# Token order for every q, k and v product: residue order is made at the splits and, for v, by a copy through DRAM

## The chip, the cores and the metric

The kernel runs on one core of one Trainium2 chip. The metric is the device time of one execution in microseconds; a kernel's time is the median over its runs.

## What is computed

The reference is a trunk of two residual layers on 512 tokens of width 1024, all in float32. Each layer normalises x, multiplies it by a wide matrix `w_in` and cuts the product into the inputs of a recurrent branch (causal convolution, RG-LRU scan, times a GeLU gate), of an attention branch (q, k, v of 12 heads of 128) and of two sigmoid gates. Both branches are projected, gated, summed, projected by `w_out` and added to x. A gated MLP (width 3072, a causal convolution of width 3 before the GeLU) follows.

The attention has three groups of four heads with dilation 1, 4 and 16. Tokens are regrouped by their residue, and inside a residue each query sees a causal window:

```python
def to_blocks(t):
    t = t.reshape(bsz, n, dilation, h, dh).transpose(0, 2, 1, 3, 4)
...
q = rotary(rms_norm(q, q_g), positions) * (HEAD_DIM ** -0.5)
k = rotary(rms_norm(k, k_g), positions)
```

Group outputs are merged by softmax weights from their denominators.

## The kernel before

**Products.** Every product is done as three float32r passes: an operand is split into a high part (rounded, by ScalarE) and a low part (the rest, by VectorE), and `mm3` (lines 258 to 260) multiplies high by high, high by low and low by high into one PSUM bank. x is held transposed as `xh`, `xl` (128 channels by 512 tokens, 8 tiles each). Weights come as 320 units of 128x1024 (`wraw`, 512 KB each, loaded by SP), and each is split into `whi` (ScalarE, line 228) and `wlo` (VectorE, line 233), both with three buffers and two units ahead of TensorE.

**Groups.** A layer's products are a fixed list of groups, each with four PSUM banks `acc`. The first nine are for attention, in the order N1, P1, v0, va, P2, N2, P3, P4, vb, of 4 units and 96 matmuls of 128x512 each. N1 and N2 are q and k of dilation 1, P1 to P4 are q and k of the dilated groups 1 and 2, v0 is v of dilation 1, va and vb are v of the dilated groups. In these nine the x tile is the stationary operand and the weights move ("acc<-whi,xh" in a profile, the moving operand named first); a bank is 128 tokens by 512 channels. In all later groups the weights are stationary ("acc<-xh,whi").

**Which tokens a bank holds.** For N1, N2 and v0 bank b takes tokens 128b to 128b+127. For P1 to P4, va and vb it takes the 128 tokens of residue b modulo 4:

```python
view = "p (r a) -> p r a" if name in IN_ORDER else "p (a r) -> p r a"
av = ah.rearrange(view, r=4)[:, b]
bv = al.rearrange(view, r=4)[:, b]
```

so the stationary operand is 128 neighbouring columns in one case and every fourth column in the other.

**After a q/k group.** `QK.bank` copies each bank to a `slot` (ScalarE). Per bank, `squares` sums the squares of each head (ScalarE), `block` multiplies by the gain, applies rotary with tables `cos`, `sns` (VectorE), scales k by its norm `rs` (two ScalarE activations of 128x128), transposes the four heads into one PSUM tile `at` (TensorE, line 264), and `split` writes the high part (ScalarE) and the low part (VectorE) into the quads `th`, `tl`. The q scale goes into the scores (`rsp` in `score_steps`, VectorE line 237). The tables, the norm `rc` and its form `rcx` exist twice, in token order and in residue order (index `o`).

**After a v group.** `V.bank` scales each bank into a quad `self.t` (ScalarE). `values_perm`, one per head s, splits two residues of va or vb at a time, transposes the probabilities and multiplies ("y<-quad", lines 794 and 795); `values_nat` does it for v0.

**Order of the work.** Engines run their queues in the order written. The order comes from a planner in the kernel: side work (rotary, scores, values, scans, splits) is cut into steps, each with an engine and a time before which it is not put into the queue, and `offer` places steps between the matmuls by running totals of estimated time per engine (`T`). `at` has two buffers; a step that needs one is placed when the estimate says that it came free 500 ns before. A group that needs a result forces what is missing (`ensure`): pa0, the sixth group after vb, needs the attention of each head.

Of the kernel before, what the change touches and what calls it, by code (L numbers as in the profile page):

```python
# [15 lines left out]
F32 = mybir.dt.float32  # L16
# [17 lines left out]
HOP = 6500.0  # L34
# [146 lines left out]
def trunk(tc, wst, lruw, xT, pos, par, gqk, cst, yT):  # L181
    from contextlib import ExitStack
    nc = tc.nc
    with ExitStack() as ctx:
# [151 lines left out]

        def split(hi, lo, src, t=0.0):
            yield need("act", t)
            t = copy(rr(hi), src, t)
            yield need("dve", t)  # L340
            return tt(rr(lo), src, hi, ALU.subtract, t)

# [88 lines left out]
        const = cp.tile([128, C_N], F32, name="const")  # L431
        posi = cp.tile([128, 8], I32, name="posi")
        warm = cp.tile([128, 1], F32, name="warm")
# [16 lines left out]

        cos = cp.tile([128, 8, 64], F32, name="cos")
        sns = cp.tile([128, 8, 2, 64], F32, name="sns")

        def rope_tables():
            yield need("dve", s=3)
            posf = small([8], "posf", 1)
            nc.vector.tensor_copy(posf, posi)
            a, k, r2 = salloc(), salloc(), salloc()
            for r in range(8):
                ts(a[:, r * 64:r * 64 + 64], const[:, C_FR:C_FR + 64], posf[:, r:r + 1], None, ALU.mult)  # L460
                on_dve(60, 0.0)
            magic = float(1.5 * 2 ** 23)
            yield need("dve")
            ts(k, a, float(1.0 / (2 * np.pi)), magic, ALU.mult, ALU.add)
            ts(k, k, -magic, None, ALU.add, dep=T["dve"])
            for p in two_pi_parts():
                yield need("dve", T["dve"])
                stt(a, k, -p, a, ALU.mult, ALU.add, T["dve"])
            yield need("dve")
            lim = 3.1415925  # L470
            t = ts(a, a, lim, -lim, ALU.min, ALU.max)
            yield need("act", t)
            t = act(r2, a, AF.Sin, scale=0.5)
            t = act(sns[:, :, 0, :], a.rearrange("p (r f) -> p r f", r=8), AF.Sin)
# [4 lines left out]
            free(a, k, r2)  # L479

# [63 lines left out]
        def norm_finish(which):  # L544
            yield need("act", s=2, after=[square[c] for c in range(8)])
            sh, sl = salloc(), salloc()
            t = copy(rr(sh), ssq, T["dve"])
            yield need("dve", t)
            t = tt(rr(sl), ssq, sh, ALU.subtract, t)
            yield need("pe", t, at=1)  # L550
            ps = bank()
            nc.tensor.matmul(ps, rr(ones), rr(sh), start=True, stop=False)
            nc.tensor.matmul(ps, rr(ones), rr(sl), start=False, stop=True)
            on_pe(512, 2)
            free(sh, sl)
# [12 lines left out]
            rv = rbc.rearrange("p (a r) -> p r a", r=4)  # L568
            for r in range(4):
                nc.tensor.transpose(pc[:, r:r + 1], rbc[0:1, r * 128:r * 128 + 128], ident[0:1, 0:1])  # L570
                nc.tensor.transpose(pc[:, 4 + r:5 + r], rv[0:1, r, :], ident[0:1, 0:1])
            on_pe(1, 8)
            yield need("dve", T["pe"])
            rc = small([8], "rc", 1)
            nc.vector.tensor_copy(rc, pc[:, 0:8])
            bank_done(on_dve(8, T["pe"]))
            rcx = small([8, 2, 2], "rcx", 1)
            ts(rcx[:, :, 0, :], rc.unsqueeze(2).to_broadcast([128, 8, 2]), -1.0, None, ALU.mult)
            ts(rcx[:, :, 1, :], rc.unsqueeze(2).to_broadcast([128, 8, 2]), 1.0, None, ALU.mult)
            scale["rc"], scale["rcx"] = rc, rcx  # L580
# [4 lines left out]
        class QK:  # L585


            def __init__(self, l, name):
                self.l, self.name = l, name
                self.g, self.left = salloc(), 4  # L590
                nc.sync.dma_start(self.g, gqk[l, list(QK_GROUPS).index(name)].partition_broadcast(128))
                self.msq = small([16], "msq", 2)
                self.o = 0 if name in IN_ORDER else 4
                self.qg = []
                self.rs_done = Chain(None, 0)
# [10 lines left out]
            def squares(self, r):  # L606
                yield need("act", after=(scale["norm"],))
                rc = scale["rc"][:, self.o + r:self.o + r + 1]
                for j in range(4):
                    junk = small([128], "junk", 1)  # L610
                    act(junk, self.qg[r][:, j * 128:j * 128 + 128], AF.Square, scale=rc, accum_out=self.msq[:, 4 * r + j:4 * r + j + 1])

            def chain(self):
# [12 lines left out]
                t = recip(sd, sd, t)  # L626
                self.t_rs = tt(rs, sd, scale["rcx"][:, self.o:self.o + 4], ALU.mult, t)
                self.rs_done.done = True
                yield need("dve", after=subs)

            def block(self, r, after):
                th, tl, rs = qkt[self.name]
                o = self.o + r
                t = self.qg[r]
# [7 lines left out]
                w = t2.rearrange("p (j h f) -> p j h f", j=4, h=2)  # L642
                tt(w, v, sns[:, o].unsqueeze(1).to_broadcast([128, 4, 2, 64]), ALU.mult, e)
                e = tt(v, v, cos[:, o].unsqueeze(1).unsqueeze(1).to_broadcast([128, 4, 2, 64]), ALU.mult, T["dve"])
# [3 lines left out]
                yield need("act", e, after=(self.rs_done,))  # L648
                e = max(e, self.t_rs)
                for j in range(2):  # L650
                    kq = t[:, (2 * j + 1) * 128:(2 * j + 2) * 128]
                    e = act(kq, kq, AF.Copy, e, scale=rs[:, r, 1, j:j + 1])
                yield need("pe", e, at=1)
# [3 lines left out]
                free(t)  # L657
                bl = slice(r * 128, r * 128 + 128)
                bank_done((yield from split(th[:, :, bl], tl[:, :, bl], ps.rearrange("p (j t) -> p j t", j=4), T["pe"])))

        class V:
# [4 lines left out]
            def bank(self, r, ps):  # L666
                o = (0 if self.name in IN_ORDER else 4) + r
                act(self.t[:, r, :], ps, AF.Copy, T["pe"], scale=scale["rc"][:, o:o + 1])

            def end(self):  # L670
                vt[self.name] = self.t
                v_done[self.name].done = True
                v_done[self.name].end = T["act"]

        def score_steps(half, s, p0, p12, st0, st12):
            hq, lq, rsn = qkt["N1" if s < 2 else "N2"]
            hp, lp, rsp = qkt[f"P{s + 1}"]
            yield need("pe", at=1)
# [3 lines left out]
            for b in bs:  # L682
# [9 lines left out]
                else:  # L692
                    for g in range(2):
                        out = ps[:, o + g * 128:o + g * 128 + 128]
                        mm3(out, hp[:, 2 * g, q], lp[:, 2 * g, q], hp[:, 2 * g + 1, q], lp[:, 2 * g + 1, q], True, True)
                        m = C_M1 + 128 * g
                        todo.append((p12[:, b, g * 128:g * 128 + 128], out, rsp[:, b, 0, g:g + 1], const[:, m:m + 128]))
            t = T["pe"]
# [5 lines left out]
            for out, src, r, m in todo:  # L704
                t = stt(out, src, r, m, ALU.mult, ALU.add, t)
            bank_done(t)
# [412 lines left out]
        for l, name, _, nk, k0, _ in GROUPS:  # L1119
# [13 lines left out]
            for uu in range(nk // 2):  # L1133
# [34 lines left out]
                for b in range(4):  # L1168
                    bs = slice(b * 128, b * 128 + 128)
                    for kk in range(2):  # L1170
# [14 lines left out]
                        if tok:  # L1185
                            view = "p (r a) -> p r a" if name in IN_ORDER else "p (a r) -> p r a"
                            av = ah.rearrange(view, r=4)[:, b]
                            bv = al.rearrange(view, r=4)[:, b]
                            ws = slice(kk * 512, kk * 512 + 512)
                            mm3(banks[b], av, bv, hi[:, ws], lo[:, ws], first, last)  # L1190
                        else:
# [38 lines left out]
```

## Time and profile before

| | |
|---|---|
| time, median of 3 runs | 1895.0 us (1894.29 to 1895.2) |
| the profiled execution | 1894.81 us |
| its span, first to last instruction | 1893.0 us |
| TensorE busy | 1881.1 us, 99% |
| TensorE weight loads | 1613.3 us, 85% |
| VectorE busy | 1218.9 us, 64% |
| ScalarE busy | 967.1 us, 51% |
| GpSimd busy | 1.9 us |
| chain that ended last | 97% TensorE, 2% ScalarE, 1% VectorE |

The span is 1.8 us shorter than the time of the same execution. PE is TensorE's matmuls, PEld its weight loads, which lie beside matmuls, DVE is VectorE, ACT ScalarE, POOL GpSimd, SP the queue that issues most transfers.

### The profile page before, as it was taken

The numbers are of one execution on the slowest core, as the hardware profiler recorded it, in microseconds if no ns is written. First come the engines' busy times: TensorE is split into PE (matmuls) and PEld (weight loads), VectorE is DVE, ScalarE is ACT, GpSimd is POOL, SyncE is SP. The second block draws the span as 40 slices with busy tenths as digits, with TensorE's granted clock in tenths as the row PEclk, the third lists the DMA queues.
The fourth block names the chain that finished last, engine by engine and source line by source line (L and its number), as shares of the span: only waits on it lengthen the run. The fifth ranks groups of instructions, "written<-read, shape, count | busy, mean of one in ns | idle before, by whom it ended". The sixth has DMA issues, their size and how long they took to land.

```text
span 1893.0 us, 22326 instructions
## 1 busy us (share of the span) xinstructions
PE 1881.1 (99%) x8624; PEld 1613.3 (85%) x8624; DVE 1218.9 (64%) x1781; ACT 967.1 (51%) x1683; POOL 1.9 (0%) x7
## 2 busy tenths in 40 slices
PE   8999999999999999999999999999999999999999
PEld 7899988888888888888889999888888888888887
DVE  6848877765456763477476488777744577636762
ACT  6758866663344441344367588666533444313431
POOL 0000000000000000000000000000000000000000
PEclk9999999999999999999999999999999999999999
DMA  5222223222322222222332232222223222222222
GB/s 174 93 76 81 87 73 101 84 90 99 141 100 90 101 100 98 92 100 94 129 107 94 84 101 70 77 101 83 95 101 138 92 98 100 100 100 90 99 102 89
DMA packets 66026, 185.69 MB, mean 98 GB/s; under 512 B 16928, under 2 KB 17056, under 8 KB 65920
## 3 DMA queue, kind: packets, MB, share of 16 engines
q1 hardware_dynamic: 61392, 183.59, 28.2%
q8 instruction: 67, 1.10, 0.2%
q10 hardware_dynamic: 4368, 0.17, 0.1%
q0 software_dynamic: 160, 0.50, 0.1%
q14 instruction: 39, 0.32, 0.1%
HBM read 180.00 MB, written 4.24 MB: 97 GB/s over the span
## 4 chain that ended last, share of the span: by engine, by line
PE 97%; ACT 2%; DVE 1%; DMA 0%; issue 0%; SPq 0%; DVEq 0%
PE acc L258 31%; PE acc L259 30%; PE acc L260 30%; PE at L264 2%; PE at L260 1%; PE at L259 1%; PE at L258 1%; ACT junk L222 1%; PE y L794 1%; DMA wraw<-wst 0%; ACT whi L228 0%; ACT slot L222 0%; PE y L795 0%; PE y L258 0%; PE y L260 0%
## 5 line engine op out<-in xcount | busy, mean ns | idle before, releaser
L228 ACT CAST whi<-wraw 128x1024 fp32r<-128x1024 f32 (+1 forms) x321 | 334.9, 1043 | 596.1 <-PE acc L259 514.6
L233 DVE TENSOR_TENSOR wlo<-wraw,whi 128x1024 fp32r<-128x1024 f32 (+1 forms) x321 | 390.5, 1217 | 270.5 <-ACT whi L228 270.3
L258 PE MATMUL acc<-xh,whi 128*128 128x512 f32 x1280 | 500.3, 391 | 0.0
L260 PE MATMUL acc<-xh,wlo 128*128 128x512 f32 x1280 | 498.2, 389 | 0.0
L259 PE MATMUL acc<-xl,whi 128*128 128x512 f32 x1280 | 498.2, 389 | 0.0
L260 PEld LDWEIGHTS acc<-xh,wlo 128*128 128x128 f32 x1280 | 240.3, 188 | 50.3
L259 PEld LDWEIGHTS acc<-xl,whi 128*128 128x128 f32 x1280 | 240.4, 188 | 49.0
L258 PEld LDWEIGHTS acc<-xh,whi 128*128 128x128 f32 x1280 | 240.3, 188 | 48.9
L258 PE MATMUL acc<-quad,whi 128*128 128x512 f32 x640 | 249.0, 389 | 0.0
L259 PE MATMUL acc<-quad,whi 128*128 128x512 f32 x640 | 249.0, 389 | 0.0
L260 PE MATMUL acc<-quad,wlo 128*128 128x512 f32 x640 | 249.0, 389 | 0.0
L258 PE MATMUL acc<-whi,xh 128*128 128x512 f32 x576 | 239.9, 416 | 7.9 <-ACT whi L228 7.9
L259 PE MATMUL acc<-wlo,xh 128*128 128x512 f32 x576 | 229.1, 398 | 0.0
L260 PE MATMUL acc<-whi,xl 128*128 128x512 f32 x576 | 228.6, 397 | 0.0
L258 PEld LDWEIGHTS acc<-whi,xh 128*128 128x128 f32 x576 | 155.8, 271 | 15.9 <-ACT whi L228 8.6
L259 PEld LDWEIGHTS acc<-wlo,xh 128*128 128x128 f32 x576 | 156.9, 272 | 8.0 <-DVE wlo L233 0.9
L260 PEld LDWEIGHTS acc<-whi,xl 128*128 128x128 f32 x576 | 155.8, 270 | 7.9
L233 DVE TENSOR_TENSOR slot<-acc,rbc 128x512 f32<-128x512 f32 x112 | 77.3, 690 | 126.3 <-PE acc L260 126.3
L260 PEld LDWEIGHTS acc<-quad,wlo 128*128 128x128 f32 x640 | 120.1, 188 | 25.0
L258 PEld LDWEIGHTS acc<-quad,whi 128*128 128x128 f32 x640 | 120.1, 188 | 24.9
L259 PEld LDWEIGHTS acc<-quad,whi 128*128 128x128 f32 x640 | 120.1, 188 | 24.9
L228 ACT CAST quad<-quad 128x512 fp32r<-128x512 f32 x80 | 49.8, 623 | 89.0 <-DVE quad L233 89.0
(137 smaller groups left out, 1946.8 us busy)
## 6 DMA issues: line engine op xcount, KB each, us to landing
wraw<-wst SPq DMA_DIRECT2D x319, 512.0 KB, 3.2
quad<-xT SPq DMA_DIRECT2D x16, 256.0 KB, 5.2
slot<-gqk SPq DMA_DIRECT2D x12, 256.0 KB, 3.6
slot<-lruw SPq DMA_DIRECT2D x8, 256.0 KB, 5.3
xdram<-quad SPq DMA_DIRECT2D x8, 256.0 KB, 3.2
quad<-xdram SPq DMA_DIRECT2D x8, 256.0 KB, 6.8
yT<-quad SPq DMA_DIRECT2D x8, 256.0 KB, 2.1
wraw<-wst SPq DMA_DIRECT2D x2, 256.0 KB, 5.6
```

Source lines behind the costliest of these rows:

```text
L222: nc.scalar.activation(out, src, func, **kw)
L228: nc.scalar.copy(out, src)
L233: nc.vector.tensor_tensor(out, a, b, op=op)
L258: nc.tensor.matmul(ps, rr(ah), rr(bh), start=first, stop=False)
L259: nc.tensor.matmul(ps, rr(ah), rr(bl), start=False, stop=False)
L260: nc.tensor.matmul(ps, rr(al), rr(bh), start=False, stop=last)
L264: nc.tensor.transpose(out, src, ident)
L794: nc.tensor.matmul(yp[:, o:o + 256].rearrange("p (k t) -> p k t", k=2), rr(w[:, 2, b]), rr(w[:, 0:2, b]), start=i == 0, stop=False)
```

## The change

All nine attention groups take 128 neighbouring tokens per bank. The residue order of groups 1 and 2 is made later: `block` reads the transposed PSUM tile with a step of four elements when it splits q and k of P1 to P4, so that each block fills 32 neighbouring columns of each residue; v of va and vb is written to DRAM from the POOL queue and read back, row p of the quad then holding tokens 4p to 4p+3. The tables and norms in residue order go away. For P1 to P4 one VectorE multiplication applies both norms (q and k) to the block before the transposes, in place of the two activations on k and of the q scale in the scores; the scores then only add the mask. The planner's estimate for the strided splits is doubled, and 2 x 6500 ns are set for v's way through DRAM.

```diff
-        def split(hi, lo, src, t=0.0):
+        def split(hi, lo, src, t=0.0, strided=False):
             yield need("act", t)
             t = copy(rr(hi), src, t)
+            if strided:
+                T["act"] = t = t + 0.834 * size(src)
             yield need("dve", t)
-            return tt(rr(lo), src, hi, ALU.subtract, t)
+            t = tt(rr(lo), src, hi, ALU.subtract, t)
+            if strided:
+                T["dve"] = t = t + 1.05 * size(src)
+            return t
...
-        cos = cp.tile([128, 8, 64], F32, name="cos")
-        sns = cp.tile([128, 8, 2, 64], F32, name="sns")
+        cos = cp.tile([128, 4, 64], F32, name="cos")
+        sns = cp.tile([128, 4, 2, 64], F32, name="sns")
...
             for r in range(4):
                 nc.tensor.transpose(pc[:, r:r + 1], rbc[0:1, r * 128:r * 128 + 128], ident[0:1, 0:1])
-                nc.tensor.transpose(pc[:, 4 + r:5 + r], rv[0:1, r, :], ident[0:1, 0:1])
...
+                if self.name in IN_ORDER:
+                    yield need("act", e, after=(self.rs_done,))
+                    e = max(e, self.t_rs)
+                    for j in range(2):
+                        kq = t[:, (2 * j + 1) * 128:(2 * j + 2) * 128]
+                        e = act(kq, kq, AF.Copy, e, scale=rs[:, r, 1, j:j + 1])
+                else:
+                    yield need("dve", e, after=(self.rs_done,))
+                    w = t.rearrange("p (j k d) -> p j k d", j=2, k=2)
+                    rq = rs[:, r].rearrange("p k j -> p j k").unsqueeze(3).to_broadcast([128, 2, 2, 128])
+                    e = tt(w, w, rq, ALU.mult, max(e, self.t_rs))
...
-                bl = slice(r * 128, r * 128 + 128)
-                bank_done((yield from split(th[:, :, bl], tl[:, :, bl], ps.rearrange("p (j t) -> p j t", j=4), T["pe"])))
+                if self.name in IN_ORDER:
+                    bl = slice(r * 128, r * 128 + 128)
+                    outs = [w[:, :, bl] for w in (th, tl)]
+                    ps = ps.rearrange("p (j t) -> p j t", j=4)
+                else:
+                    outs = [w.rearrange("p j (q b a) -> p j q b a", q=4, b=4)[:, :, :, r] for w in (th, tl)]
+                    ps = ps.rearrange("p (j a q) -> p j q a", j=4, q=4)
+                bank_done((yield from split(*outs, ps, T["pe"], self.name not in IN_ORDER)))
...
+                if self.name not in IN_ORDER:
+                    d = dr.tile([S, 512], F32, name="vorder", tag="vorder", bufs=2)
+                    nc.gpsimd.dma_start(d.rearrange("(b p) c -> p b c", p=128), self.t)
+                    nc.gpsimd.dma_start(self.t, d.rearrange("(p r) c -> p r c", r=4))
+                    v_done[self.name].end += 2 * HOP
...
-                        todo.append((p12[:, b, g * 128:g * 128 + 128], out, rsp[:, b, 0, g:g + 1], const[:, m:m + 128]))
+                        todo.append((p12[:, b, g * 128:g * 128 + 128], out, None, const[:, m:m + 128]))
...
-                            view = "p (r a) -> p r a" if name in IN_ORDER else "p (a r) -> p r a"
-                            av = ah.rearrange(view, r=4)[:, b]
-                            bv = al.rearrange(view, r=4)[:, b]
+                            ts_ = slice(b * 128, b * 128 + 128)
                             ws = slice(kk * 512, kk * 512 + 512)
-                            mm3(banks[b], av, bv, hi[:, ws], lo[:, ws], first, last)
+                            mm3(banks[b], ah[:, ts_], al[:, ts_], hi[:, ws], lo[:, ws], first, last)
```

**Place 1: VectorE, one block of P1 in layer 0.** Of before, from the low part of one block's split to that of the next:

```order
L233 TENSOR_TENSOR quad<-at,quad 128x4x128
L233 TENSOR_TENSOR slot<-slot 128x512
L233 TENSOR_TENSOR slot<-slot,sns 128x512
L233 TENSOR_TENSOR slot<-slot,cos 128x512
L233 TENSOR_TENSOR slot<-slot 128x4x64 x2
L233 TENSOR_TENSOR quad<-at,quad 128x4x128
```

Of the change, the same place:

```order
L233 TENSOR_TENSOR quad<-at,quad 128x16x32
L233 TENSOR_TENSOR slot<-slot,rsP_628 128x512
L233 TENSOR_TENSOR slot<-slot 128x512
L233 TENSOR_TENSOR slot<-slot,sns 128x512
L233 TENSOR_TENSOR slot<-slot,cos 128x512
L233 TENSOR_TENSOR slot<-slot 128x4x64 x2
L233 TENSOR_TENSOR quad<-at,quad 128x16x32
```

One multiplication by the norms (`rsP`) has come in per block, and the low part is written in 16 pieces of 32 columns.

**Place 2: ScalarE, from the end of va in layer 0 to the first reading of its quad.** Here `quad<-acc,rc` empties a bank of va, `whi<-wraw` is the high part of a weight unit, and the first `CAST quad<-quad 128x512` reads va. Of before:

```order
L222 ACTIVATE quad<-acc,rc 128x512
L222 ACTIVATE quad<-quad,f 128x256 x4
L222 ACTIVATE quad<-acc,rc 128x512
L228 CAST whi_82<-wraw 128x1024
L228 CAST slot<-quad 128x512
L228 CAST quad<-at 128x512
L228 CAST quad<-quad 128x512
```

Of the change:

```order
L222 ACTIVATE quad<-acc,rc 128x512 x2
L228 CAST whi_82<-wraw 128x1024
L222 ACTIVATE e_1086<-e_1086 128x8
L222 ACTIVATE quad<-quad,f 128x256 x4
L228 CAST whi_83<-wraw 128x1024
L228 CAST whi_84<-wraw 128x1024
L228 CAST quad<-at 128x512
L228 CAST slot<-quad 128x512
L228 CAST quad<-quad 128x512
```

The reading stands behind three weight units instead of one; it waits for the second of va's two DMAs.

**Place 3: the POOL queue.** Of the change, from the loads at the program's start on:

```order
L445 DMA prm_130<-par 128x272
L690 DMA vorder<-quad 128x4x512
L691 DMA quad<-vorder 128x2048
L690 DMA vorder<-quad 128x4x512
L691 DMA quad<-vorder 128x2048
L690 DMA vorder<-quad 128x4x512
L691 DMA quad<-vorder 128x2048
L690 DMA vorder<-quad 128x4x512
L691 DMA quad<-vorder 128x2048
```

Eight transfers of 1 MB have come in, two for each of va and vb in each layer; nothing else stands in this queue behind the start.

## Rows read from the trace of the kernel before

**Rows 1.** The page: the span, busy time by engine, and the clock that TensorE was granted in 40 slices of the span.

```profile
span 1893.0 us, 22326 instructions
PE 1881.1 (99%) x8624; PEld 1613.3 (85%) x8624; DVE 1218.9 (64%) x1781; ACT 967.1 (51%) x1683; POOL 1.9 (0%) x7
PEclk9999999999999999999999999999999999999999
```

**Rows 2.** Waits of TensorE's matmuls and weight loads over the whole span: engine, line, what it waited for, us in total, times, longest.

```profile
PE acc L258 <- ACT whi L228: 7.9, 2, 6.0
PE at L264 <- ACT slot L222: 0.2, 1, 0.2
PEld acc L259 <- DVE wlo L233: 0.9, 2, 0.4
```

**Rows 3.** Instructions grouped by line and shape: one of the three passes of the nine attention groups and of the later groups, matmul and weight load. Behind the count stand busy us, mean ns of one, and idle time before them.

```profile
L259 PE MATMUL acc<-xl,whi 128*128 128x512 f32 x1280 | 498.2, 389 | 0.0
L259 PE MATMUL acc<-wlo,xh 128*128 128x512 f32 x576 | 229.1, 398 | 0.0
L259 PEld LDWEIGHTS acc<-xl,whi 128*128 128x128 f32 x1280 | 240.4, 188 | 49.0
L259 PEld LDWEIGHTS acc<-wlo,xh 128*128 128x128 f32 x576 | 156.9, 272 | 8.0 <-DVE wlo L233 0.9
```

**Rows 4.** Timeline of TensorE in P1 of layer 0 (every fourth column stationary): start, duration. The first and the last matmul of 59 in a row with nothing between them, and one weight load.

```profile
44.33 0.40 PE L259 MATMUL acc<-wlo,xh 128*128 128x512 f32 x1
...
57.96 0.40 PE L260 MATMUL acc<-whi,xl 128*128 128x512 f32 x1
...
44.57 0.31 PEld L258 LDWEIGHTS acc<-whi,xh 128*128 128x128 f32 x1
```

**Rows 5.** The same in N1 of layer 0 (neighbouring columns): the first and the last of 60 in a row, and one weight load.

```profile
20.44 0.39 PE L258 MATMUL acc<-whi,xh 128*128 128x512 f32 x1
...
33.81 0.40 PE L260 MATMUL acc<-whi,xl 128*128 128x512 f32 x1
...
20.44 0.19 PEld L259 LDWEIGHTS acc<-wlo,xh 128*128 128x128 f32 x1
```

**Rows 6.** Timeline of TensorE where four transposes (L264) stand between the matmuls of a group: the matmul before them, the transposes, and the twelfth matmul after them. First in P2 (every fourth column), then in v0 (neighbouring columns).

```profile
113.43 0.39 PE L260 MATMUL acc<-whi,xl 128*128 128x512 f32 x1
113.67 0.60 PE L264 MATMUL at<-const,quad 128*128 128x128 f32 x4
...
116.81 0.40 PE L260 MATMUL acc<-whi,xl 128*128 128x512 f32 x1
...
67.17 0.39 PE L260 MATMUL acc<-whi,xl 128*128 128x512 f32 x1
67.40 0.60 PE L264 MATMUL at<-const,slot 128*128 128x128 f32 x4
...
70.38 0.39 PE L260 MATMUL acc<-whi,xl 128*128 128x512 f32 x1
```

**Rows 7.** Timeline of TensorE: the first row of the first and of the last of 46 places at which other work stands between two matmuls of one of the groups P1 to P4, va and vb, both layers counted.

```profile
34.75 0.39 PE L552 MATMUL at<-slot,ones 128*128 128x512 f32 x1
...
1183.83 0.60 PE L264 MATMUL at<-const,slot 128*128 128x128 f32 x4
```

**Rows 8.** Timeline of TensorE: the first and the last of the eight transposes of the norm in layer 0, and the matmul behind them.

```profile
43.05 0.22 PE L570 MATMUL at<-const,rbc 1*128 1x1 f32 x1
...
43.68 0.25 PE L571 MATMUL at<-const,rbc 1*128 1x1 f32 x1
43.86 0.63 PE L258 MATMUL acc<-whi,xh 128*128 128x512 f32 x1
```

**Rows 9.** ScalarE and VectorE groups by shape, columns as in rows 3: the splits' high and low part, a copy of half the elements that writes every fourth element and the addition behind it (both for `y`), the activations that scale k, and a VectorE product of two SBUF operands.

```profile
L228 ACT CAST quad<-at 128x512 fp32r<-128x512 f32 x64 | 36.3, 583 | 10.8 <-PE at L264 10.6
L228 ACT COPY slot<-y 128x256 f32<-128x256 f32 x16 | 10.0, 627 | 21.8 <-PE y L795 21.8
L222 ACT ACTIVATE slot<-slot,rsP 128x128 f32<-128x128 f32 x64 | 21.2, 394 | 5.0 <-DVE rsP L233 4.7
L233 DVE TENSOR_TENSOR quad<-at,quad 128x512 fp32r<-128x512 f32 x64 | 42.4, 684 | 15.7 <-ACT quad L228 15.7
L233 DVE TENSOR_TENSOR slot<-slot,y 128x256 f32<-128x256 f32 x16 | 10.1, 634 | 25.7 <-ACT slot L228 25.7
L233 DVE TENSOR_TENSOR slot<-slot,sns 128x512 f32<-128x512 f32 x48 | 33.2, 692 | 1.7
```

**Rows 10.** Busy time by engine in three stretches: length, PE, PEld, DVE, ACT, POOL (with counts), granted clock, DMA share, GB/s. The first two lie in the attention stage (P2 to P4 of layer 0), the third is the busiest for DMA in its surroundings (eight loads of x behind one another).

```profile
142.00:190.00 48.00, 48.00 (x238) 44.32 (x237) 40.62 (x80) 42.74 (x122) 0.00 (x0) 1.00 0.25 83
190.00:237.00 47.00, 47.00 (x244) 46.46 (x244) 40.05 (x70) 40.75 (x117) 0.00 (x0) 1.00 0.25 87
500.00:505.00 5.00, 5.00 (x23) 4.14 (x23) 1.23 (x1) 0.44 (x1) 0.00 (x0) 1.00 0.96 372
```

**Rows 11.** DMA issues: what, queue, count, KB each, median us from issue to landing. The second is one of three that POOL issues at the start.

```profile
wraw<-wst SPq DMA_DIRECT2D x319, 512.0 KB, 3.2
const<-cst POOLq DMA_DIRECT2D x1, 352.0 KB, 6.3
```

More of the change, by code (lines that the diff above doesn't have):

```diff
@@ L431, in trunk @@
         const = cp.tile([128, C_N], F32, name="const")
-        posi = cp.tile([128, 8], I32, name="posi")
+        posi = cp.tile([128, 4], I32, name="posi")
         warm = cp.tile([128, 1], F32, name="warm")
@@ L448, in trunk @@
         eps1, eps128 = bias[:, 0:1], bias[:, 1:2]
-        cos = cp.tile([128, 8, 64], F32, name="cos")
-        sns = cp.tile([128, 8, 2, 64], F32, name="sns")
+        cos = cp.tile([128, 4, 64], F32, name="cos")
+        sns = cp.tile([128, 4, 2, 64], F32, name="sns")
         def rope_tables():
             yield need("dve", s=3)
-            posf = small([8], "posf", 1)
+            posf = small([4], "posf", 1)
             nc.vector.tensor_copy(posf, posi)
-            a, k, r2 = salloc(), salloc(), salloc()
-            for r in range(8):
+            slots = salloc(), salloc(), salloc()
+            a, k, r2 = (w[:, 0:256] for w in slots)
+            for r in range(4):
                 ts(a[:, r * 64:r * 64 + 64], const[:, C_FR:C_FR + 64], posf[:, r:r + 1], None, ALU.mult)
@@ L473, in rope_tables @@
             t = act(r2, a, AF.Sin, scale=0.5)
-            t = act(sns[:, :, 0, :], a.rearrange("p (r f) -> p r f", r=8), AF.Sin)
+            t = act(sns[:, :, 0, :], a.rearrange("p (r f) -> p r f", r=4), AF.Sin)
             yield need("dve", t)
@@ L478, in rope_tables @@
             ts(sns[:, :, 1, :], sns[:, :, 0, :], -1.0, None, ALU.mult)
-            free(a, k, r2)
+            free(*slots)
         sp4 = cp.tile([128, L, 2, 8], F32, name="sp4")
@@ L567, in norm_finish @@
             pc = bank()
-            rv = rbc.rearrange("p (a r) -> p r a", r=4)
             for r in range(4):
                 nc.tensor.transpose(pc[:, r:r + 1], rbc[0:1, r * 128:r * 128 + 128], ident[0:1, 0:1])
-                nc.tensor.transpose(pc[:, 4 + r:5 + r], rv[0:1, r, :], ident[0:1, 0:1])
-            on_pe(1, 8)
+            on_pe(1, 4)
             yield need("dve", T["pe"])
[L574 to L579, printed above, removed]
+            rc = small([4], "rc", 1)
+            nc.vector.tensor_copy(rc, pc[:, 0:4])
+            bank_done(on_dve(4, T["pe"]))
+            rcx = small([4, 2, 2], "rcx", 1)
+            ts(rcx[:, :, 0, :], rc.unsqueeze(2).to_broadcast([128, 4, 2]), -1.0, None, ALU.mult)
+            ts(rcx[:, :, 1, :], rc.unsqueeze(2).to_broadcast([128, 4, 2]), 1.0, None, ALU.mult)
             scale["rc"], scale["rcx"] = rc, rcx
@@ L592, in __init__ @@
                 self.msq = small([16], "msq", 2)
-                self.o = 0 if name in IN_ORDER else 4
                 self.qg = []
@@ L607, in squares @@
                 yield need("act", after=(scale["norm"],))
-                rc = scale["rc"][:, self.o + r:self.o + r + 1]
+                rc = scale["rc"][:, r:r + 1]
                 for j in range(4):
@@ L626, in chain @@
                 t = recip(sd, sd, t)
-                self.t_rs = tt(rs, sd, scale["rcx"][:, self.o:self.o + 4], ALU.mult, t)
+                self.t_rs = tt(rs, sd, scale["rcx"], ALU.mult, t)
                 self.rs_done.done = True
@@ L642, in block @@
                 w = t2.rearrange("p (j h f) -> p j h f", j=4, h=2)
-                tt(w, v, sns[:, o].unsqueeze(1).to_broadcast([128, 4, 2, 64]), ALU.mult, e)
-                e = tt(v, v, cos[:, o].unsqueeze(1).unsqueeze(1).to_broadcast([128, 4, 2, 64]), ALU.mult, T["dve"])
+                tt(w, v, sns[:, r].unsqueeze(1).to_broadcast([128, 4, 2, 64]), ALU.mult, e)
+                e = tt(v, v, cos[:, r].unsqueeze(1).unsqueeze(1).to_broadcast([128, 4, 2, 64]), ALU.mult, T["dve"])
                 tt(v[:, :, 0, :], v[:, :, 0, :], w[:, :, 1, :], ALU.add, e)
@@ L647, in block @@
                 free(t2)
[L648 to L652, printed above, removed]
+                if self.name in IN_ORDER:
[9 more added lines that the diff above has]
+                    e = tt(w, w, rq, ALU.mult, max(e, self.t_rs))
                 yield need("pe", e, at=1)
@@ L666, in bank @@
             def bank(self, r, ps):
-                o = (0 if self.name in IN_ORDER else 4) + r
-                act(self.t[:, r, :], ps, AF.Copy, T["pe"], scale=scale["rc"][:, o:o + 1])
+                act(self.t[:, r, :], ps, AF.Copy, T["pe"], scale=scale["rc"][:, r:r + 1])
             def end(self):
@@ L673, in end @@
                 v_done[self.name].end = T["act"]
+                if self.name not in IN_ORDER:
[3 more added lines that the diff above has]
+                    v_done[self.name].end += 2 * HOP
         def score_steps(half, s, p0, p12, st0, st12):
             hq, lq, rsn = qkt["N1" if s < 2 else "N2"]
-            hp, lp, rsp = qkt[f"P{s + 1}"]
+            hp, lp, _ = qkt[f"P{s + 1}"]
             yield need("pe", at=1)
@@ L704, in score_steps @@
             for out, src, r, m in todo:
-                t = stt(out, src, r, m, ALU.mult, ALU.add, t)
+                t = tt(out, src, m, ALU.add, t) if r is None else stt(out, src, r, m, ALU.mult, ALU.add, t)
             bank_done(t)
@@ L1217 @@
         "xT": np.ascontiguousarray(w["x"][0].T),
-        "pos": np.ascontiguousarray(np.concatenate([w["positions"].reshape(4, 128).T, w["positions"].reshape(128, 4)], axis=1)),
+        "pos": np.ascontiguousarray(w["positions"].reshape(4, 128).T),
         "par": pack_params(w),
```

1 line of the change is left out of this document (removed).

## The prediction

> **What bounds the kernel now.** I read the page first. TensorE is busy for 1881.1 of 1893.0 us and its clock is granted in full in every slice, that is at 2.4 GHz; VectorE and ScalarE are at 64% and 51% [rows 1]. Then the waits: TensorE's matmuls wait 7.9 us at the start, for the first weights, and 0.2 us once later; nothing else holds them [rows 2]. So the side engines set the end only where they make TensorE wait, and today they never do. The question is what a matmul costs, and then whether the side engines still keep up.
>
> A matmul's row lasts 389 ns in the later groups and 398 ns on average in the nine attention groups, and its weight load 188 and 272 ns [rows 3]. These means mix two layouts, and durations of pipelined matmuls overlap, so I went to the timeline and took the distance between starts. In P1, where the stationary operand is every fourth column, 58 steps take 57.96 - 44.33 = 13.63 us, 235.0 ns each, and a weight load lasts 0.31 us [rows 4]. In N1, with neighbouring columns, 59 steps take 33.81 - 20.44 = 13.37 us, 226.6 ns each, and a load 0.19 us [rows 5]. Same engine, same clock, same shape, same moving operand: only the step of the stationary operand differs. A load of 0.31 us can still be hidden in a stream, but not for free.
>
> **The change, part by part.**
>
> *Products.* P1 to P4, va and vb in two layers are 12 groups of 96 matmuls, 1152 in all. 1152 x (235.0 - 226.6) ns = 9.7 us less.
>
> *Interruptions.* Where side work stands between two matmuls, TensorE has to get its loads ahead again. From the matmul before four transposes to the twelfth behind them it takes 116.81 - 113.43 = 3.38 us in P2 and 70.38 - 67.17 = 3.21 us in v0 [rows 6]. Of the difference of 0.17 us, 12 x 8.4 ns = 0.10 are counted already; 0.07 us remain per interruption. There are 46 [rows 7]: 46 x 0.07 = 3.2 us less. Longer interruptions may cost more than this pair shows. If all cost twice that, it would be 6.4 us; if the surplus goes with the length of the insert rather than with the layout, nothing.
>
> *Norm.* Four of eight transposes of the norm fall away per layer. The eight take 43.86 - 43.05 = 0.81 us to the next matmul [rows 8]; half of it, twice, is 0.8 us less.
>
> *VectorE and ScalarE.* Per block of P1 to P4 (16 per layer) VectorE gets one product of 128x512, which is nearest to the rotary row's 0.69 us [rows 9], and ScalarE loses two activations of 0.39. The splits now read PSUM with a step of four. No row shows that. Bounds: nothing, that is 583 and 684 ns as now (the same elements in wider steps have no reason to come faster); and, from the rows of y, whose half-size copy and addition step by four in SBUF and take 627 and 634 ns, twice that, 1254 and 1268 ns [rows 9]. I take the upper one, since it steps by the same four words. VectorE then gets 0.69 + 0.58 = 1.27 us per block, 20 us per layer; ScalarE 0.67 - 0.79 = 0.1 us less. What hides this: in the two fullest stretches VectorE is busy for 40.6 of 48 and 40.1 of 47 us, ScalarE for 42.7 and 40.8 [rows 10]. A stretch of 48 us holds about two groups; if both are P groups that is 8 blocks and 10 us more for VectorE against 7.4 us free. Taken alone this doesn't fit, but the planner counts the doubled splits and puts the surplus off: it has until pa0, five groups after vb. So I cost it at nothing; without that cover the missing 2.6 us fall on each pair of P groups, four pairs in two layers, 10 us in all. The scores lose a factor and keep their instruction count. An `at` bank is held 0.67 + 0.58 = 1.25 us longer per block; the planner places the next user behind its estimate plus 500 ns.
>
> *v through DRAM.* Two transfers of 1 MB (1.05 MB) follow each other per va and vb. Nothing else queues behind them on POOL. What waits is ScalarE's reading of the quad, and behind it on ScalarE stand the emptying of the next group's banks and the split of the weights, for which TensorE waits. Lower bound: a weight unit of 0.52 MB lands 3.2 us after its issue [rows 11], of which 1.4 us go at the 372 GB/s that a full stretch shows [rows 10], so 1.8 us are fixed; 1.05 MB need 2.8 + 1.8 = 4.6 us, two of them 9.2. Upper bound: POOL's own load at the start needed 6.3 us for 0.36 MB [rows 11], 5.3 of them fixed, so 8.1 and 16.2. The cover: the reading stands behind the third weight unit after va's last bank. With three `whi` buffers that unit's split begins when TensorE is done with the second unit of P2, 48 x 0.2266 = 10.9 us after va's end; with that split (1.05), an `at` copy and a v0 split (0.6 each) it is 13.1 us. For vb the probabilities' scaling stands there too, and I put it at 15. I take 9.2 to 12 us for the trip, since the upper bound comes from a start in which everything loads at once: no wait. At 16.2 ScalarE would wait 3.1 and 1.2 us, 8.6 us in two layers.
>
> The Trainium skill warns of this path. Its page "SBUF — State Buffer", section "SBUF: two separate sides", says that a DMA issued from the POOL queue has its descriptors written by the GpSimd cores, and that these are locked out while VectorE runs in a two-port mode. Its section "Who interferes with whom" says that `tensor_tensor` has no such mode. Nearly all VectorE rows of this stage are `tensor_tensor`, so by the second rule nothing is added and the sum stays, and by the first alone the trip grows and the time is that of the second rival below; no run here shows POOL issuing beside a busy VectorE.
>
> **Sum.** 9.7 + 3.2 + 0.8 = 13.7 us less. The profiled execution took 1894.81 us, 0.2 below the median: 1881.1 by its own time, 1881.3 by the median. I predict 1881 us.
>
> **Rivals.**
>
> *The gain is partly eaten.* v's trip takes its upper bound (8.6 us), or VectorE falls behind in the P groups (10 us). For it: VectorE at 85% with 20% more to do per group. Against: TensorE waited for either engine 0.2 us in all after the start today [rows 2]. One of the two leaves 1895.0 - 13.7 + 8.6 = 1890 us or 1891; a half of one 1886.
>
> *v comes much too late, and the kernel gets slower.* The place is ScalarE's first reading of va and of vb, four times in the program. It decides at 13.7 / 4 = 3.4 us of waiting each, so at a trip of some 17.5 us. At 20 us ScalarE waits 6.9 and 5 us, 23.8 in all: 1895 + 10 = 1905 us. For it: VectorE is idle for only 15% of these stretches, if POOL needs that idle time, and the weights load at 83 to 87 GB/s beside it [rows 10]. Against: the POOL upper bound of 16.2 us stays below.
>
> *The products don't get faster.* If a load were wholly hidden behind the matmul before it, the layout would not matter and only the norm's 0.8 us and any new wait would show: 1894 us. Against it stand the two steps of 235.0 and 226.6 ns [rows 4, 5]. The Trainium skill, "TensorE: Matmul & The Clock Gate", section "Step-by-step: what each phase is for", speaks for it: the next load runs while this matmul does, through a port of its own, and its time goes with the column count. The trace disagrees in the last point, 0.31 against 0.19 us for 128 columns each.
>
> *More gain.* All interruptions cost twice what the pair shows: 1878 us.
>
> **How the numbers follow.** My forecast (1878 to 1884) has 0.70, the eaten gain (1884 to 1891) 0.13, products not faster or a gain eaten whole (1891 to 1899) 0.07, v too late 0.10. The measurement tells 0.2%, 3.8 us, from no change. Faster by more than that is below 1891.2: 0.70 + 0.13 = 0.83; same 0.07; slower 0.10. The range that holds 8 in 10 goes from 1877, one us below the case of more gain, to 1891, the end of the eaten gain. For the likeliest case alone it is 1878 to 1884.
>
> **What would show it.** Right: one form of weight load near 188 ns and one of matmul near 389 ns in all attention groups; starts 226.6 ns apart in P1; TensorE's waits still below 1 us after the start; ScalarE waiting for `quad<-vorder` not at all or below 1 us; v's two transfers landing within 6 us each. Wrong: rows in which ScalarE waits for `vorder`, or TensorE for `at` or `acc` copies, with several us; a split of 128x16x32 above 1.3 us; P groups still at 235 ns.

## The result, and the profile after

The changed kernel takes 1905.55 us (1902.8 to 1909.45, four runs) against 1894.83 us before: ratio 1.0059 [1.0047, 1.0072], 10.7 us slower. The forecast was 1881 us.

The page of after, span, engines and clock, to be held against [rows 1]:

```profile
span 1903.8 us, 22297 instructions
PE 1875.5 (99%) x8616; PEld 1557.1 (82%) x8616; DVE 1232.6 (65%) x1809; ACT 945.4 (50%) x1619; POOL 7.1 (0%) x15
PEclk9999999999999999999999999998999999999999
```

TensorE is busy for 5.6 us less while the span is 10.8 us longer, so it stands still. One slice shows less than the full clock. Waits of TensorE's matmuls after, columns as in [rows 2]:

```profile
PE acc L258 <- DVE quad L233: 13.4, 2, 6.7
PE acc L258 <- ACT whi L228: 7.2, 2, 6.1
PE at L264 <- ACT slot L222: 1.6, 1, 1.6
PE at L559 <- DVE slot L233: 1.5, 1, 1.5
PE at L264 <- DVE slot L233: 0.8, 3, 0.3
```

The second row is the wait at the start that before has too. The first is new: two waits of 6.7 us for VectorE. The timeline of TensorE after, around the first of them (start, duration, idle time before and its releaser); it stands between the last matmul of ga0, the group ahead of pa0, and the first of pa0 in layer 0:

```profile
376.47 0.39 PE L260 MATMUL acc<-xh,wlo 128*128 128x512 f32 x1
383.57 0.77 PE L258 MATMUL acc<-slot,whi 128*128 128x512 f32 x1 [6.71 <-DVE quad L233]
384.13 0.63 PE L259 MATMUL acc<-slot,whi 128*128 128x512 f32 x1
384.56 0.63 PE L260 MATMUL acc<-slot,wlo 128*128 128x512 f32 x1
...
388.83 0.42 PE L258 MATMUL acc<-slot,whi 128*128 128x512 f32 x1
389.09 0.39 PE L259 MATMUL acc<-slot,whi 128*128 128x512 f32 x1
389.32 0.40 PE L260 MATMUL acc<-slot,wlo 128*128 128x512 f32 x1
```

Behind the wait twelve matmuls start 0.44 us apart on average, then they come 0.23 us apart again: after 6.7 us of idling TensorE ran at the lower of its two levels, 1.2 GHz, for 388.83 - 383.57 = 5.3 us, and 12 x 0.227 = 2.7 us would have done. In windows of after (columns as in [rows 10]) it is the granted clock below 1, and 0.50 in the first microsecond after the wait:

```profile
377.00:384.00 7.00, 0.43 (x1) 0.46 (x2) 4.84 (x9) 2.35 (x4) 0.00 (x0) 0.86 0.00 0
383.00:384.00 1.00, 0.43 (x1) 0.46 (x2) 1.00 (x3) 0.50 (x1) 0.00 (x0) 0.50 0.00 0
384.00:398.00 14.00, 14.00 (x53) 11.24 (x53) 7.42 (x11) 6.46 (x9) 0.00 (x0) 0.83 0.26 84
398.00:420.00 22.00, 22.00 (x99) 18.23 (x98) 16.60 (x23) 14.85 (x23) 0.00 (x0) 1.00 0.26 90
```

The stop costs 6.9 us (383.57 - 376.47 less one step of 0.23) and the clock 2.6: 9.5 us, and as much in layer 1, 19 us in all. Without them the kernel would be at about 1886.5 us, an estimate from these rows, and faster than before.

**What VectorE does meanwhile.** pa0's first matmul needs a PSUM bank that ga0 filled, and VectorE empties it. Its timeline after:

```profile
376.01 1.28 DVE L233 TENSOR_TENSOR quad<-quad 128x512 fp32r<-128x512 f32 x2
377.98 1.29 DVE L233 TENSOR_TENSOR quad<-quad 128x512 fp32r<-128x512 f32 x2 [0.69 <-ACT quad L228]
379.95 1.29 DVE L233 TENSOR_TENSOR quad<-quad 128x512 fp32r<-128x512 f32 x2 [0.69 <-ACT quad L228]
381.93 0.69 DVE L233 TENSOR_TENSOR quad<-quad 128x512 fp32r<-128x512 f32 x1 [0.68 <-ACT quad L228]
382.73 1.29 DVE L233 TENSOR_TENSOR quad<-acc,rbc 128x512 f32<-128x512 f32 x2
```

And of before:

```profile
376.55 1.28 DVE L233 TENSOR_TENSOR quad<-quad 128x512 fp32r<-128x512 f32 x2
379.62 0.69 DVE L233 TENSOR_TENSOR quad<-quad 128x512 fp32r<-128x512 f32 x1 [1.79 <-ACT quad L228]
380.42 1.29 DVE L233 TENSOR_TENSOR quad<-acc,rbc 128x512 f32<-128x512 f32 x2
```

`quad<-acc,rbc` is the emptying. In the changed kernel it stands behind a ping-pong with ScalarE: a product of the recurrent branch, ScalarE's high part of it, the low part, 1.97 us a round. That is the tail of the chain that multiplies the recurrent branch by its GeLU gate (called gr0's chain here, after the group that computes the gate). It stands there because of the pool of work tiles:

```python
while not quads:     # qalloc
    force()          # pushes the oldest chain that can go on
```

There are 11 quads (`NQ`). ga0's `Gate` claims one when the group's last weight unit begins, before any of its banks is emptied. None is free, so `force` puts the oldest step that can go on into the queues until a chain gives its quads back. By a count in the planner it pushes 2 steps per layer there in the kernel before and 11 in the changed one. In the rows above seven steps of gr0's chain stand on VectorE ahead of the emptying after, and three before.

**Theories.** (1) Side work is later than before, since the planner counts the doubled splits; at ga0 no quad is free, and the pushed chain runs ahead of the emptying. (2) v's trip through DRAM makes ScalarE, and all behind it, late. (3) VectorE has too much to do ahead of pa0.

### The profile page after: what moved, and what is told of

Read it like the earlier page. It is cut to its first block, busy times and chain, and to the rows that moved or that the text cites. A ratio compares the mean times of both kernels' runs of the same rounds, so it can differ in the third digit from the quotient of the medians.

```text
span 1903.8 us, 22297 instructions
## 1 busy us (share of the span) xinstructions
PE 1875.5 (99%) x8616; PEld 1557.1 (82%) x8616; DVE 1232.6 (65%) x1809; ACT 945.4 (50%) x1619; POOL 7.1 (0%) x15
## 4 chain that ended last, share of the span: by engine, by line
PE 93%; ACT 3%; DVE 3%; DMA 1%; issue 0%; SPq 0%; DVEq 0%; ACTq 0%
PE acc L258 29%; PE acc L259 29%; PE acc L260 29%; PE at L264 2%; ACT junk L222 1%; DVE quad L233 1%; PE at L259 1%; PE at L260 1%; PE at L258 1%; PE y L813 0%; DVE quad L900 0%; ACT quad L222 0%; ACT whi L228 0%; DVE wlo L233 0%; DMA stats<-st 0%
## 5 line engine op out<-in xcount | busy, mean ns | idle before, releaser
L233 DVE TENSOR_TENSOR wlo<-wraw,whi 128x1024 fp32r<-128x1024 f32 (+1 forms) x321 | 390.6, 1217 | 254.1 <-ACT whi L228 253.8
L258 PE MATMUL acc<-xh,whi 128*128 128x512 f32 x1280 | 500.7, 391 | 0.0
L258 PEld LDWEIGHTS acc<-xh,whi 128*128 128x128 f32 x1280 | 240.4, 188 | 48.9
L258 PE MATMUL acc<-quad,whi 128*128 128x512 f32 x640 | 249.0, 389 | 0.0
L258 PE MATMUL acc<-whi,xh 128*128 128x512 f32 x576 | 232.2, 403 | 7.2 <-ACT whi L228 7.2
L259 PE MATMUL acc<-wlo,xh 128*128 128x512 f32 x576 | 226.6, 393 | 0.0
L233 DVE TENSOR_TENSOR slot<-acc,rbc 128x512 f32<-128x512 f32 x112 | 77.2, 690 | 116.6 <-PE acc L260 116.6
L258 PEld LDWEIGHTS acc<-quad,whi 128*128 128x128 f32 x640 | 120.1, 188 | 24.9
L258 PEld LDWEIGHTS acc<-whi,xh 128*128 128x128 f32 x576 | 109.3, 190 | 28.5 <-ACT whi L228 7.9
L260 PEld LDWEIGHTS acc<-whi,xl 128*128 128x128 f32 x576 | 109.1, 189 | 23.7
L259 PEld LDWEIGHTS acc<-wlo,xh 128*128 128x128 f32 x576 | 109.2, 190 | 21.4 <-DVE wlo L233 0.9
```

Source lines behind the costliest of these rows:

```text
L233: nc.vector.tensor_tensor(out, a, b, op=op)
L258: nc.tensor.matmul(ps, rr(ah), rr(bh), start=first, stop=False)
L259: nc.tensor.matmul(ps, rr(ah), rr(bl), start=False, stop=False)
L260: nc.tensor.matmul(ps, rr(al), rr(bh), start=False, stop=last)
```

## The experiments

**The quad claimed early.**

```diff
+                if kind == "ga" and uu == 0:
+                    early["q"] = qalloc()
...
-                self.t = qalloc() if wide else []
+                self.t = early.pop("q") if wide else []
```

> The changed kernel with one edit: the quad that group ga0 (and ga1) writes its gates to is taken at the group's first weight unit and not at its last, so that what has to be finished to free one is queued three units earlier. Theory 1 (at ga0 no quad is free, so gr0's chain of product and split is queued ahead of the emptying of ga0's banks; TensorE waits 6.7 us per layer at pa0 and then runs at the lower clock, 2.6 us per layer): both go, 2 x 9.3 = 18.6 us, so about 1887 us, and no wait of several us at pa0. Theory 2 (v's way through DRAM, 12 to 14 us, holds ScalarE and all behind it): nothing changes, 1905 us. Theory 3 (VectorE has too much to do in the P groups, wherever it is put): most of the loss stays, 1900 us or more.

Measured: 1886.47 us, ratio 0.9961 [0.9946, 0.9976]. TensorE no longer waits at pa0. Theory 1 holds. The execution that was profiled took 1891.3 us, the other three 1885.75 to 1886.84. It has one other wait, 3.3 us for VectorE ahead of four transposes at 263 us. VectorE in turn had stood idle until a small transfer of the softmax statistics landed:

```profile
258.90 0.17 DVE L233 TENSOR_TENSOR mx<-stp,st 128x4 f32<-128x4 f32 x1 [6.79 <-DMA stp<-stats]
```

The last experiment comes back to it.

**No surcharge in the planner.** The instructions stay, only the estimate goes back to that of the plain split.

```diff
-            if strided:
-                T["act"] = t = t + 0.834 * size(src)
...
-            if strided:
-                T["dve"] = t = t + 1.05 * size(src)
```

> The changed kernel without the planner's doubled estimate for the splits that read PSUM with a step of four; all operations stay. In the trace of the changed kernel these splits last 583 and 686 ns, as the plain ones do, so the estimate put work off for nothing. Theory 1: rotary, scores and recurrence come earlier, gr0's chain is nearly done when ga0 wants its quad, as before the change; 1887 us and no long wait at pa0. Theory 2: 1905 us. Theory 3: VectorE gets the same work in less room, so waits in the P groups, 1905 us or more.

Measured: 1885.23 us, ratio 0.9949 [0.9935, 0.9964], the lowest median of all versions that do the whole computation. Its waits of TensorE:

```profile
PE acc L258 <- ACT whi L228: 7.0, 2, 5.8
PE at L264 <- ACT slot L222: 2.4, 2, 1.6
PE at L264 <- DVE slot L233: 0.7, 2, 0.3
PE at L555 <- DVE slot L233: 0.6, 1, 0.6
```

Two terms of an estimate, and no operation, were worth 20 us. Theory 3 falls: VectorE's work is the same here (1809 instructions, busy for 1231.0 us against 1232.6).

**v without its trip.** v of va and vb stays in token order, so the attention of groups 1 and 2 is not the reference's; the planner's 13 us stay.

```diff
-                    nc.gpsimd.dma_start(d.rearrange("(b p) c -> p b c", p=128), self.t)
-                    nc.gpsimd.dma_start(self.t, d.rearrange("(p r) c -> p r c", r=4))
```

> The changed kernel without the two transfers of va and vb; the planner's 13 us for them and every other instruction stay where they are. v is left in token order, so the part of the attention of groups 1 and 2 that weighs v is not the reference's. Theory 1: the same waits at pa0, 1905 us. Theory 2: ScalarE no longer waits, 1881 to 1895 us. Contention of these transfers with the weights, if it costs anything, shows as the difference to the changed kernel.

Measured: 1904.19 us, ratio 1.005 [1.0035, 1.0065], with the same row, "PE acc L258 <- DVE quad L233: 13.4, 2, 6.7". Theory 2 falls.

**The product term alone.** The kernel before with neighbouring tokens as the stationary operand in all nine groups (so groups 1 and 2 mix tokens), and nothing else.

```diff
-                            view = "p (r a) -> p r a" if name in IN_ORDER else "p (a r) -> p r a"
+                            view = "p (r a) -> p r a"
```

> The kernel before with one edit: P1 to P4, va and vb take neighbouring tokens as the stationary operand, and nothing else changes (so q, k, v of groups 1 and 2 stand in the wrong order for what follows). This measures the product term alone. If it was right: 9.7 + 3.2 = 12.9 us less than before, 1882 us. If loads are hidden behind the matmul before them: 1895 us.

Measured: 1883.21 us, ratio 0.9938 [0.9922, 0.9955], 11.5 us less. The first matmul of layer 1 and the last of the program, in timelines of the kernel before, of this one and of the one without surcharge:

```profile
951.37 0.39 PE L258 MATMUL acc<-whi,xh 128*128 128x512 f32 x1
...
1888.86 0.39 PE L260 MATMUL acc<-quad,wlo 128*128 128x512 f32 x1
```

```profile
945.72 0.39 PE L258 MATMUL acc<-whi,xh 128*128 128x512 f32 x1
...
1877.13 0.39 PE L260 MATMUL acc<-quad,wlo 128*128 128x512 f32 x1
```

```profile
947.31 0.39 PE L258 MATMUL acc<-whi,xh 128*128 128x512 f32 x1
...
1879.02 0.39 PE L260 MATMUL acc<-quad,wlo 128*128 128x512 f32 x1
```

Layer 1 takes 937.49, 931.41 and 931.71 us: products and interruptions save 6.1 us there, and the whole change without the surcharge 5.8. In layer 0, from the first matmul on (6.02, 5.83 and 5.85 us), it is 945.35, 939.89 and 941.46: 5.5 us saved by the products, only 3.9 by the change. The short waits of the version without surcharge go with that, since 3.3 of their 3.7 us fall in layer 0. That they are all of it is not shown: the kernel of this experiment has 1.9 us of short waits in layer 0 too.

**A twelfth quad.**

```diff
-NQ = 11
+NQ = 12
```

> The changed kernel with a twelfth quad and nothing else: the planner's surcharge stays, no tile is claimed earlier. Theory 1 (at ga0 no quad is free, so the oldest chain is pushed ahead of the emptying of ga0's banks): the claim succeeds at once, pa0's first matmul no longer waits 6.7 us on VectorE in either layer, the clock stays granted in full, and the time falls by 2 x (6.7 + 2.6) = 18.6 us to 1887 us (1884 to 1891). Theory 3 (VectorE simply has too much work before pa0): one more quad makes no work fall away, so the wait at pa0 stays and the time is 1900 to 1906 us.

Measured: 1886.4 us, ratio 0.9958 [0.9941, 0.9975]. Surcharge, work and place of the claim are as changed, and 19.2 us are gone, against 18.6 expected. VectorE at the same place:

```profile
377.69 0.69 DVE L233 TENSOR_TENSOR quad<-acc,rbc 128x512 f32<-128x512 f32 x1
378.29 0.68 DVE L233 TENSOR_TENSOR quad<-quad 128x512 fp32r<-128x512 f32 x1
378.89 0.68 DVE L233 TENSOR_TENSOR quad<-acc,rbc 128x512 f32<-128x512 f32 x1
```

The same late `quad<-quad` now stands between the emptyings instead of ahead of all of them.

**Slower products put back.** The stationary operand of P1 to P4, va and vb again takes every fourth token (their tokens come in the wrong order for what follows).

```diff
+                            if name not in IN_ORDER:
+                                av, bv = (w.rearrange("p (a r) -> p r a", r=4)[:, b] for w in (ah, al))
```

> The changed kernel whose q, k and v products of groups 1 and 2 read every fourth token again as the stationary operand; everything behind the products is as changed, so those groups' tokens come in the wrong order for it and its output is not the reference's. With neighbouring tokens the kernel before became 11.5 us shorter. If that price adds to the rest, this kernel is 11 us slower than the changed one, 1916 us (1912 to 1920). If instead the slower products give the side engines time, so that the wait at pa0 shrinks, it stays at 1905 us or falls below: the two waits of 6.7 us hold up to 18.6 us that longer products could use as cover.

Measured: 1917.91 us, ratio 1.0129 [1.0114, 1.0144], 12.4 us above the changed kernel. The two waits at pa0 stay as they were, 6.70 us each against 6.71. Longer products don't fill them.

**The surcharge alone, on the kernel before.**

```diff
+            if strided:
+                T["act"] = t = t + 0.834 * size(src)
...
+            if strided:
+                T["dve"] = t = t + 1.05 * size(src)
```

> The kernel before, instruction for instruction the same work, with only the planner's surcharge on the splits of P1 to P4 (0.43 us for ScalarE and 0.54 us for VectorE per split that do not exist). If wrong planning numbers alone are enough to make TensorE wait, the order of the side work moves later here too; the planner then pushes 4 chains per layer ahead at the quad's claim before pa0 (2 without the surcharge, 11 in the changed kernel), so a wait of up to 2 to 3 us per layer, 1895 to 1901 us. If it takes the changed operations too (fuller VectorE, shorter products) the time is 1895 us and no acc wait shows at pa0.

Measured: 1899.41 us, ratio 1.0025 [1.0015, 1.0035], 4.8 us slower for the same operations in another order. Only ScalarE's table loads are more, 38 instead of 34. Its waits:

```profile
PE acc L258 <- ACT whi L228: 7.8, 2, 6.3
PE acc L258 <- DVE quad L233: 1.3, 2, 0.7
PE at L264 <- ACT slot L222: 0.3, 1, 0.3
PE y L800 <- DVE quad L233: 0.2, 1, 0.2
```

The wait at pa0 is there, at a tenth of its size. Only 1.6 of the 4.8 us are rows of new waits; the rest was not located. The wrong number does harm by itself; for the full size of the harm the other parts of the change are needed beside it, and which of them was not tested.

**Early claim and no surcharge together.** The edits of the first two experiments.

> The changed kernel with both remedies: ga0's quad claimed at ga0's first unit, and no surcharge on the strided splits. Theory 1: the surcharge alone already removed both waits (1885.2 us), so the early claim adds at most what the 2 pushed chains per layer still cost, under 1 us: 1883 to 1886 us. If the early claim itself costs something (it takes a quad from the attention chains 22 us earlier, and with it the changed kernel waited 3.3 us on VectorE in front of transposes), it is 1886 to 1889 us.

Measured: 1892.41 us, ratio 0.9988 [0.9978, 0.9997], 7.2 us worse than without the surcharge alone. A matmul of the recurrent gates waits in ga0 of each layer for the high part that ScalarE makes:

```profile
364.66 0.39 PE L260 MATMUL acc<-xh,wlo 128*128 128x512 f32 x1
366.84 0.50 PE L258 MATMUL at<-slot,quad 128*128 128x512 f32 x1 [1.79 <-ACT slot L228]
367.56 0.50 PE L259 MATMUL at<-slot,quad 128*128 128x512 f32 x1 [0.22 <-DVE slot L233]
367.90 0.39 PE L260 MATMUL at<-slot,quad 128*128 128x512 f32 x1
```

The three steps from 364.66 to 367.90 us take 3.24 us, and at 0.227 each they would take 0.68: 2.6 us more, which is what each layer is longer around it. Two remedies for one shortage need not add: each moves the order.

**Twelve quads and no surcharge.**

> The changed kernel without the surcharge and with a twelfth quad, which was worth 19.2 us as a remedy of its own. If the surcharge had only acted through the quads, both remedies together give no more than the first alone, 1885.2 us: 1884 to 1886. If the free quad also removes what the 2 pushed chains per layer still cost without the surcharge, it is 1882 to 1884. If more free tiles move other work together, as the early claim did beside the missing surcharge (1892.4 us), it is 1887 to 1893.

Measured: 1886.46 us, ratio 0.9955 [0.9942, 0.9967], against [0.9935, 0.9964] without the surcharge alone: the two can't be told apart. Once the order is right, a free quad has nothing left to give.

**No surcharge and no trip of v.** As in the third experiment, the attention of groups 1 and 2 is not the reference's.

> The changed kernel without the surcharge and without v's two transfers through DRAM per va and vb; the planner's 13 us for them stay. v stays in token order there, so the attention of groups 1 and 2 is not the reference's. It prices the trip in a program that doesn't wait at pa0. If the trip is hidden, as the prediction costed it, the time is that of the kernel without the surcharge, 1885.2 us within 0.7. If the transfers slow the weights beside them or hold ScalarE, it is shorter by that: up to 5 us, 1880 us.

Measured: 1885.77 us, ratio 0.9951 [0.9938, 0.9965], against 1885.23 with the trip. The trip is hidden in the median time. It is not free for what is in flight beside it: at vb of layer 0 the statistics' write of 4 KB (`stats<-st`) lands after 6.9 us in the changed kernel and after 3.1 without the trip. In the profiled execution with the early claim it took 7.1 us and the reading back 5.2, and VectorE's idle time shown there ended with that landing. That this made that execution the slowest of its four was not tested.

## Why the prediction was wrong, point by point

**The step that failed** is the one on VectorE and ScalarE: "the planner counts the doubled splits and puts the surplus off: it has until pa0, five groups after vb. So I cost it at nothing". Two things are wrong in it. The surplus isn't there: a strided split costs nothing extra. The groups by shape after, to [rows 9]:

```profile
L228 ACT CAST quad<-at 128x512 fp32r<-128x512 f32 x64 | 36.4, 583 | 27.1 <-PE at L264 27.1
L233 DVE TENSOR_TENSOR quad<-at,quad 128x512 fp32r<-128x512 f32 x64 | 42.8, 686 | 15.6 <-ACT quad L228 15.4
L233 DVE TENSOR_TENSOR slot<-slot,rsP 128x512 f32<-128x512 f32 x32 | 21.5, 686 | 0.3
```

583 and 686 ns are the lower bound, and I took the upper, from a row that steps by four in SBUF. (The first two rows mix 32 strided splits with 32 others; twice the time for the strided ones would show in the mean.) And putting off is not free: I took pa0's `ensure` for the only deadline. But postponed work holds its tiles, and the claim of a quad at ga0 is a deadline too, for the recurrent branch, which the change doesn't touch. What is pushed there stands in VectorE's queue ahead of the emptying of the banks. Taking the surcharge away, adding a quad or claiming earlier removes the wait each by itself; that is as much as these runs can show of the cause.

**The lower clock** was no term at all. It adds 2.6 us to each stop.

**Products and interruptions** were right in kind: weight loads in one form of 190 ns, matmuls 393 ns on average (403 in the first pass, where the matmul right behind side work lasts longer), no step of 235 ns. The two terms, 12.9 us, measured 11.5 by the times, and 12.2 as twice layer 1. After, as in [rows 3]:

```profile
L259 PE MATMUL acc<-wlo,xh 128*128 128x512 f32 x576 | 226.6, 393 | 0.0
L259 PEld LDWEIGHTS acc<-wlo,xh 128*128 128x128 f32 x576 | 109.2, 190 | 21.4 <-DVE wlo L233 0.9
```

The rival that saw no gain in the products falls with them.

**The norm's 0.8 us** came, as 1.0. After, the four transposes of layer 1 and the matmul behind them:

```profile
974.76 0.40 PE L575 MATMUL at<-const,rbc 1*128 1x1 f32 x4
975.09 0.50 PE L258 MATMUL acc<-whi,xh 128*128 128x512 f32 x1
```

That is 0.33 us instead of 0.81 [rows 8], 0.48 less in each layer.

**Part of the gain was eaten** even without the surcharge: with the norm's 0.5 us added to the products' 5.5 and 6.1, 2.0 us are missing in layer 0 and 0.8 in layer 1. **Layer 0's first groups** hold nearly all of the 3.9 us of short waits for VectorE and ScalarE in the changed kernel (last three rows of waits). I had looked only at the stretches from 142 us on. In layer 1 the interruptions are more: counted as in [rows 7], there are 29 places without the surcharge and 20 before, where the prediction took their number as fixed. That these nine cost the 0.8 us was not tested.

**v through DRAM** cost no time, as forecast, but by luck of the bounds. Its transfers land after 6.6 and 6.2 us, 12.8 together, above the 9.2 to 12 that I took and above the 6 us each that I named as a sign of being right:

```profile
vorder<-quad POOLq DMA_DIRECT2D x4, 1024.0 KB, 6.6
quad<-vorder POOLq DMA_DIRECT2D x4, 1024.0 KB, 6.2
```

The cover was enough: the four trips took 11.4 to 14.1 us, ScalarE first read each quad 2.8 to 4.3 us after its landing, among ScalarE's waits none is for `vorder`, and without the trip nothing is gained. The Trainium skill, "SBUF — State Buffer", section "Who interferes with whom", says that `tensor_tensor` has no two-port mode and, with both inputs in SBUF, contends with GpSimd's reads. The time came out as without contention: with VectorE busy for 25 to 76% of a trip, none grew to the 20 us of the second rival.

**That rival** named 1905 us, and 1905.55 came, but the match is chance: the mechanism and the place are others. The wait is at pa0, for VectorE, and behind work that has nothing to do with v. The gain partly eaten, 1884 to 1891 us, is what the change gives once the order is repaired by one remedy: 1885.2 to 1886.5 us. Of the two causes that I gave for it, v's trip is out, and of VectorE falling behind in the P groups only short waits are seen.

## What to carry to other kernels

An estimate in a scheduler is a change to the kernel: a cost set too high "to be safe" moves work later, and whatever that work holds (tiles, banks, buffers) is missing elsewhere. When work is said to be put off, list everything that it holds until it is done, and each place that claims one of those, as deadlines. Where a pool runs dry just ahead of the emptying of a PSUM bank, what is forced there stands ahead of the emptying, and TensorE can be made to wait for it: not at all with 2 steps here, 0.7 us with 4, 6.7 us with 11.

## What the runs showed of the hardware

ScalarE and VectorE read PSUM with a step of four fp32 elements as fast as in order (583 and 686 ns for 128x512, against 583 and 684). For a weight load the same step cost 0.31 instead of 0.19 us, and the matmuls behind it 235.0 instead of 226.6 ns [rows 4, 5]. After a stop of 6.7 us TensorE ran at 1.2 GHz for 5.3 us; after a stop of 0.7 us (the surcharge alone) its next matmuls started 0.23 to 0.30 us apart, so no lower level shows there. In between it is not settled: a wait of 1.6 us in v0 of layer 0 was followed by a granted clock of 0.65 from 60 to 64 us in the changed kernel, and by the full clock in the version without the surcharge. Small transfers slowed down beside large ones: 4 KB landed after 6.9 us beside a write of 1 MB, and after 3.1 us at the same place without it.
